# A two-layer attention and state-space kernel: first group's transposes into other banks and later, output rows asked for earlier, one dt product into a score buffer

## The chip, the cores and the metric

The kernel runs on one core of a Trainium2 chip. A core has five engines that run side by side, each with a queue of its own that is worked off in order: TensorE (PE; its weight loads are shown as PEld), VectorE (DVE), ScalarE (ACT), GpSimd (POOL) and SyncE (SP), which in this kernel issues most of the DMA transfers. Matrix products are written to PSUM, eight banks of 512 fp32 columns on 128 partitions; DVE and ACT read them from there into SBUF. The metric is the device time of one execution in microseconds (us).

## The reference

The model has two layers on a latent grid of 1024 tokens and a context of 256 tokens, 1024 features each. Layer 0 is gated windowed attention with 16 heads on 4 key heads, layer 1 a bidirectional state-space scan (Mamba-2) with 8 groups of 4 heads. Both are of the form below.

```
shift, scale, gate = adaln(c, w_ada[i], b_ada[i])
u = rms_normalize(h) * (1.0 + scale) + shift
y = mixer(u, uc)
h = h + gate * y
```

The attention mixer ends with `(o * silu(g)) @ w_out`. The scan's front is a product, a convolution over five neighbours in time, and a step size per head:

```
z, xbc, dt_raw = split(h @ w_in)
xbc = silu(centred_depthwise_conv(xbc, conv_w, conv_b))
xs, bm, cm = split(xbc)
dt = softplus(dt_raw + dt_bias)
```

In each group the scan runs over chunks of 128 tokens, forwards and backwards; its states start from the final states of the context.

## The kernel before, in words

Activations lie transposed, features on the partitions and tokens in the free dimension, in three parts (`TT`): part 0 and part 1 are the first and last 512 latent tokens, part 2 the 256 of the context. Every fp32 operand x is split into a high part and a remainder (`uH` and `uL` for activations, `wh` and `wl` for weights), and a product is three matmuls, high by high, high by low and low by high (`mm3`, lines 238 to 240). A weight tile comes by DMA into `wr`; ACT makes `wh` (line 221 or 1141), POOL or DVE makes `wl` (line 223 or 1145). The program is written as one stream of Python calls; a scheduler with a simulated clock then orders each engine's instructions by readiness and priority, and `issue_after` ties an instruction to one before it on its engine.

**Attention** (`attention`, lines 818 to 961). Units of one key head and one block of 128 queries are worked off in three phases: part 2, part 0, part 1. `att_front` makes the scores in the S buffers (two, of two banks each) and asks for the unit's gate `sgt`; `att_back` transposes the probabilities and multiplies with the values (lines 793 to 800), calling `tick` after each block of keys. Each tick may call `advance`, which takes one step of a generator from the list `fill` of the phase, as filler for TensorE: in phases 2 and 0 the projections of q and gate of part 1 (`qg1`), in phase 1 the output projections of parts 2 and 0 (`out_steps`). `cur` is the running generator, `nxt` the one whose weights have been asked for. `tick` paces the steps: after `seen` of `count` ticks the share `seen/count` of the `total` steps is to be done; phase 1 has 97 steps and 76 ticks. An output tile (`one`, line 847) asks for its weights, yields, asks for its row `h1` (line 854, two buffers; eight for part 1), makes the product in 4 or 8 steps, adds the gated product to the row (line 858), stores it (859) and sums its squares. `norm` (868) turns the sums into 1/rms on all partitions: `sums` on TensorE, scale and power, a diagonal matrix on DVE (line 378) and the spreading product with ones (line 380), copied by ACT (382). `mod` (874) reloads a row (879) into an `h1` buffer and makes `uH` and `uL` from it (`modulate`, lines 299 to 301). Between phases 0 and 1 the pool of the projections closes and the pool `op` of the output rows opens (line 936).

In the attention stage the PSUM tile `pj` has one buffer: a second product in `pj` starts when the first has been read.

**After attention** (lines 943 to 961) the eight output tiles of part 1 follow one another, alternating between `pj` and S; then the two products with the dt weights (`dt_raw`, which adds the bias on ACT, line 1031, into `dts`), and the norm and modulation of part 1.

**The scan's front** (`front`, line 1128). For each group four weight tiles are worked off in the order bT, first and second half of x, cT. Each makes a product of 1024 columns in an accumulator `raw` (tag pj2, two buffers, line 1212); all but cT also make one of 256 columns for the context in `psD` (one bank, line 1197). In the first group the third dt product (1222) and the chain of dt steps (`dt_chain`) come in between. The steps behind a product wait in the queue `post`: the convolution's `taps` (1111, 1115), `silu` (1126, 1124), and `natural` (line 1160), which transposes the result on TensorE (1166) and has ACT copy it into SBUF (1167). `natural` writes the transposes over `raw` or `psD` again, or, where `apart` is set, into a `psX` buffer (three banks, which the scan uses from the first slot on, and which the dt steps use in the first group); in `before` only the second half of x is `apart`. Its steps fall due LATE (3.0 us) or, apart, LAST (6.8 us) of TensorE cost later. The chain `states` (1300), which carries the states over the chunks, starts when the second half of x is done.

Of the kernel before, what the change touches and what calls it, by code (L numbers as in the profile page):

```python
# [17 lines left out]
P = 128  # L18
# [95 lines left out]
class Kernel:  # L114
# [251 lines left out]
    def rstd_n(self, pool, pn, n, width, size=512, rout=None, dout=None, scalar=False):  # L366

        nc, t, ps = self.nc, self.t, self.psA
        nb = n // P
        rc = t(pool, [P, 4], F32, "rc", 2)[:, :nb]  # L370
        nc.scalar.activation(rc, pn[:, :nb], AF.Identity, bias=self.eps, scale=1.0 / width)
        nc.gpsimd.tensor_tensor(rc, rc, self.half.broadcast_to([P, nb]), op=ALU.pow)
        dg = t(*(dout or (pool, [P, 512], F32, "sqt"))).rearrange("p (b n) -> p b n", b=4)[:, :nb]
        if scalar:
            for b in range(nb):
                nc.scalar.activation(dg[:, b], self.ident, AF.Copy, scale=rc[:, b : b + 1])
        else:
            nc.vector.tensor_tensor(dg, self.ident.unsqueeze(1).broadcast_to([P, nb, P]), rc.unsqueeze(2).broadcast_to([P, nb, P]), op=ALU.mult)
        pr = t(ps, [P, 512], F32, self.ptag)
        self.spread_mm = nc.tensor.matmul(pr[:, :n], self.ones, dg.rearrange("p b n -> p (b n)"), start=True, stop=True)  # L380
        r = t(*(rout or (pool, [P, size], F32, f"rr{size}")))[:, :n]
        nc.scalar.copy(r, pr[:, :n])
        return r
# [434 lines left out]
    def attention(self, c0, ckv):  # L818
# [23 lines left out]
        def out_steps(i):  # L842
# [4 lines left out]
            def one(m):  # L847
                p = self.po
                w = self.load_halves(a["wo"][m], nc.gpsimd, i == 1)
                yield  # L850
                h1 = t(self.o1, [P, n], F32, "h1k") if i == 1 else t(p, [P, n], F32, "h1")
                if i == 1:
                    st[m] = h1
                nc.sync.dma_start(h1, self.xin(i)[m * P : (m + 1) * P, :])
                out = []
# [11 lines left out]

            def norm():
                p = self.po
                rout = (p, [P, n], F32, "ut" if i == 2 else "sqa")  # L870
                st["r"] = self.rstd_c(p, st["acc"], n, D, rout=rout, dout=(p, [P, 512], F32, "dg0"))
                self.alloc_u(i)
# [9 lines left out]
            def fin():  # L882
                yield
                for f in steps:
                    f()
# [22 lines left out]
        def advance(i, after):  # L908
            nonlocal cur, nxt
            with self.tc.high_priority(offset=-300), self.tc.issue_after(after):  # L910
                if cur is None:
                    cur = nxt or fill[i].pop(0)()
                    if nxt is None:
                        next(cur)
                    nxt = None
                    if fill[i]:
                        nxt = fill[i].pop(0)()
                        next(nxt)
                if next(cur, "end") == "end":
                    cur = None  # L920
# [8 lines left out]
        for x, (i, j, b) in enumerate(units):  # L929
            if oH[i] is None:  # L930
                if i == 1:
# [4 lines left out]
                    self.po = self.pool("op", ctx=c0)  # L936
                n = TT[i][1]
# [12 lines left out]
        with ExitStack() as c1:  # L950
# [6 lines left out]
            for i, lo in ((2, 256), (0, 0)):  # L957
                n = TT[i][1] // 2
                self.dt_raw(self.dts[:, lo : lo + n], self.proj(ps, self.wdt, i), n)
            for _ in steps[-1]():  # L960
                pass
# [166 lines left out]
    def front(self, g, st, post, first=None, dt=None):  # L1128
# [50 lines left out]

        tiles = [(16 + g, "bT"), (2 * g, 0), (2 * g + 1, 1), (24 + g, "cT")]  # L1180
# [7 lines left out]
        for n, (x, kind) in enumerate(tiles):  # L1188
# [4 lines left out]
            def ctx():  # L1193
# [6 lines left out]
                post.extend(self.taps(x, cr, acc, 0, CTX, CTX) + self.silu(cr, acc) + natural(cr, acc, [(st[nat[0]][2], 0, 2)], nat[1], 2))  # L1200
# [25 lines left out]
            if nat:  # L1226
                post.extend(natural(raw, acc, [(st[nat[0]][i], 4 * i, 4 * i + 4) for i in range(2)], nat[1], 8, kind == 1))
# [4 lines left out]
            post.append((LAST if kind == 1 else LATE, [done]) if nat else done)  # L1232
# [582 lines left out]
```

## Time and profile before

| | |
|---|---|
| median of three runs | 1773.27 us (1772.14 to 1777.59) |
| profiled execution: time | 1775.01 us |
| profiled execution: span in the profile | 1773.2 us |
| mean granted TensorE clock | 0.997 |
| moved by DMA | 225.53 MB, mean 127 GB/s |

| stage | from, us | to, us |
|---|---|---|
| norm, q, k, v, gate of layer 0 | 0 | 250 |
| attention, phases 2 and 0 | 250 | 490 |
| attention, phase 1 | 490 | 690 |
| output tiles of part 1, dt products | 690 | 734 |
| front of the first group | 734 | 826 |
| eight groups of scan, with the next front or the output product beside it | 826 | 1660 |
| rest of the output product and final norm | 1660 | 1773 |

The page's first part gives for each engine its busy time, its share of the span, and its instructions. A row of the table of stretches gives the stretch, its length, then for PE, PEld, DVE, ACT and POOL the busy us with the number of instructions, then the granted clock of TensorE (1.00 is full speed), the share of the DMA engines and GB/s. A row of waits gives engine, tile and line of the one who waited, engine, tile and line of the one who released it, the total in us, how often, and the longest. A row of a timeline gives the start and length in us, engine, line, operation, out<-in with sizes and the count, and in brackets the idle time before it with what ended it; SPq is SP's DMA queue. In a row of groups the numbers behind the bar are busy us, mean ns of one, and the idle time before them.

### The profile page before, as it was taken

To read this page: it belongs to the slowest core of one execution; us is meant where nothing else is said; L and a number is where in the kernel's file an instruction comes from. 1 tells how busy PE (TensorE), PEld (TensorE's weight loads), DVE (VectorE), ACT (ScalarE), POOL (GpSimd) and SP (SyncE) were. 2 spreads that over 40 slices of the span, in tenths; PEclk is the share of its full clock that TensorE was granted. 3 is DMA by queue.
4 is the path that set the end of the run, shared out by engine and by line. 5 is a ranking of instruction groups with operands and counts; after the bars stand their busy time and mean duration, and the time that the engine had idled before them with its cause. 6 is when DMAs were issued, how large, how long until landed. Compare 5 with 4: busy or idle time off the path is not lost.

```text
span 1773.2 us, 29238 instructions
## 1 busy us (share of the span) xinstructions
PE 1736.4 (98%) x10413; PEld 1503.1 (85%) x10413; DVE 1198.7 (68%) x2119; ACT 871.4 (49%) x1902; POOL 794.9 (45%) x1066
## 2 busy tenths in 40 slices
PE   9999999999999999999999999999999999999997
PEld 6897788888888887778898998989889898988887
DVE  5744436788867775694876867677686767876634
ACT  4522247777777774452544434344444434544522
POOL 3231046555565545104454554636455363554321
PEclk9999999999999999999999999999999999999999
DMA  9478856444455436222223232332333333655533
GB/s 361 169 211 271 287 146 144 102 113 97 113 153 131 119 101 223 75 69 63 76 78 96 74 92 71 86 79 74 91 81 82 83 83 80 182 164 168 179 104 119
DMA packets 211389, 225.53 MB, mean 127 GB/s; under 512 B 15788, under 2 KB 149036, under 8 KB 211244
## 3 DMA queue, kind: packets, MB, share of 16 engines
q1 hardware_dynamic: 177180, 205.02, 38.9%
q0 software_dynamic: 34064, 18.65, 5.8%
q8 instruction: 82, 1.34, 0.3%
q14 instruction: 63, 0.52, 0.1%
HBM read 188.78 MB, written 35.13 MB: 126 GB/s over the span
## 4 chain that ended last, share of the span: by engine, by line
PE 85%; DVE 7%; DMA 3%; ACT 2%; issue 2%; POOL 0%; SPq 0%; DVEq 0%; ACTq 0%; POOLq 0%
PE pj L1212 19%; PE pj L1246 10%; PE pj L1647 7%; PE pj L238 7%; PE pj L239 6%; PE pj L240 6%; PE psD L1197 4%; PE psX L1399 3%; PE pt L793 3%; PE psD L1315 2%; PE pv L800 2%; PE pv L799 2%; PE S L767 2%; PE psX L1368 2%; PE psX L1367 2%
## 5 line engine op out<-in xcount | busy, mean ns | idle before, releaser
L238 PE MATMUL pj<-uH,wh 128*128 128x512 f32 (+1 forms) x680 | 244.3, 360 | 4.2 <-DVE h L858 2.5
L239 PE MATMUL pj<-uL,wh 128*128 128x512 f32 (+1 forms) x680 | 231.0, 340 | 0.4 <-POOL uL L816 0.4
L240 PE MATMUL pj<-uH,wl 128*128 128x512 f32 (+1 forms) x680 | 230.2, 339 | 1.1 <-POOL wl L223 1.1
L1212 PE MATMUL pj<-uH,wh 128*128 128x512 f32 x512 | 173.6, 411 | 1.2 <-ACT bn L1167 1.2
L1212 PE MATMUL pj<-uH,wl 128*128 128x512 f32 x512 | 170.2, 403 | 0.0
L1212 PE MATMUL pj<-uL,wh 128*128 128x512 f32 x512 | 168.1, 402 | 0.0
L1290 POOL TENSOR_TENSOR xw<-xn,dtdec 128x256 f32<-128x256 f32 x144 | 95.6, 665 | 159.2 <-PE psD L1315 75.8
L238 PEld LDWEIGHTS pj<-uH,wh 128*128 128x128 f32 x680 | 129.6, 191 | 28.7 <-ACT wh L221 5.3
L1246 PE MATMUL pj<-wh,uH 128*128 128x256 f32 x512 | 150.5, 294 | 0.0
L1246 PE MATMUL pj<-wl,uH 128*128 128x256 f32 x512 | 150.2, 293 | 0.0
L1246 PE MATMUL pj<-wh,uL 128*128 128x256 f32 x512 | 149.9, 293 | 0.0
L798 DVE TENSOR_TENSOR pl<-pt,ph 128x512 fp32r<-128x512 f32 x168 | 115.0, 689 | 48.5 <-ACT ph L797 46.9
L240 PEld LDWEIGHTS pj<-uH,wl 128*128 128x128 f32 x680 | 129.3, 191 | 16.8 <-POOL wl L223 1.6
L239 PEld LDWEIGHTS pj<-uL,wh 128*128 128x128 f32 x680 | 130.0, 191 | 10.6 <-issue 1.1
L772 DVE CUSTOM_DVE_ANT_0 sm<-S,mask,nsink 128x640 f32<-128x640 f32 (+2 forms) x160 | 119.1, 773 | 23.4 <-PE S L768 16.9
L223 POOL TENSOR_TENSOR wl<-wr,wh 128x512 fp32r<-128x512 f32 x74 | 96.9, 1312 | 80.6 <-ACT wh L221 73.0
L1431 ACT ACTIVATE uT<-psX,nw 128x128 f32<-128x128 f32 x128 | 46.6, 364 | 170.7 <-PE psX L1430 169.8
L774 ACT ACTIVATE sm<-sm,nm 128x640 f32<-128x640 f32 (+2 forms) x160 | 118.6, 743 | 18.2 <-DVE nm L772 17.6
L797 ACT CAST ph<-pt 128x512 fp32r<-128x512 f32 x168 | 97.9, 585 | 50.9 <-PE pt L793 48.3
L221 ACT CAST wh<-wr 128x512 fp32r<-128x512 f32 (+1 forms) x116 | 74.7, 648 | 87.9 <-PE pj L239 66.1
L1212 PEld LDWEIGHTS pj<-uH,wl 128*128 128x128 f32 x512 | 95.8, 188 | 20.0
L1212 PEld LDWEIGHTS pj<-uL,wh 128*128 128x128 f32 x512 | 95.3, 188 | 19.3
(352 smaller groups left out, 4930.8 us busy)
## 6 DMA issues: line engine op xcount, KB each, us to landing
wr<-w_x SPq DMA_DIRECT2D x32, 512.0 KB, 3.8
M<-acs SPq DMA_DIRECT2D x64, 256.0 KB, 5.2
bw<-acs SPq DMA_DIRECT2D x64, 256.0 KB, 5.3
wr<-w_sk SPq DMA_DIRECT2D x24, 512.0 KB, 4.0
wr<-wg SPq DMA_DIRECT2D x40, 256.0 KB, 5.0
qs<-q POOLq DMA_DIRECT2D x40, 256.0 KB, 3.8
wada<-w_ada SPq DMA_DIRECT2D x16, 512.0 KB, 8.5
wr<-wq SPq DMA_DIRECT2D x32, 256.0 KB, 3.4
```

What stands on the lines that cost most here:

```text
L223: (eng or nc.vector).tensor_tensor(l, raw, h, op=ALU.subtract)
L238: self.nc.tensor.matmul(ps, lh, rh, start=first and i == 0, stop=False)
L239: self.nc.tensor.matmul(ps, lh, rl, start=False, stop=False)
L240: self.last_mm = self.nc.tensor.matmul(ps, ll, rh, start=False, stop=last and i == n - 1)
L772: nc.vector.tensor_tensor_reduce(out=sm[:, :W], in0=Sv, in1=self.mask[:, m0 : m0 + W], scale=-SCALE, scalar=self.nsink[:, 4 * j + r : 4 * ...
L774: nc.scalar.activation(sm[:, :W], sm[:, :W], AF.Exp, bias=nm[:, r : r + 1], scale=-1.0, accum_out=sums[:, r : r + 1])
L797: nc.scalar.copy(ph, ptf)
L798: nc.vector.tensor_sub(pl, ptf, ph)
L1212: self.pe = nc.tensor.matmul(raw[:, 512 * i : 512 * i + 512], l[:, k, :], r[i][:, k, :], start=k + y == 0, stop=k == KT - 1 and y == 2)
L1246: self.pe = nc.tensor.matmul(pj[:, c], l, r[:, k, :], start=c % 2 + q + k + y == 0, stop=c % 2 == 1 and q == 1 and k == 3 and y == 2)
L1290: nc.gpsimd.tensor_tensor(xw, X(st, c).rearrange("p (r h) -> p r h", r=R), self.dtdec[:, c, hd(d, g)].unsqueeze(2).broadcast_to([P, R, HP] ...
L1647: self.pe = nc.tensor.matmul(banks[x], l[:, z, sl], r, start=k == 2 * qs[0] and y == 0, stop=k == 2 * qs[-1] + 1 and y == 2)
```

## The change

It has four parts.

- `rstd_n` is split into `rstd_d` (up to the diagonal) and `rstd_r` (spread and copy). For part 1, `fin` now makes the sums and the diagonal at its first step. That step is taken right behind the first dt product, and the second dt product goes to an S buffer.
- An output tile has one more yield, so that its row `h1` can be asked for before its product. `advance` takes two steps of the next generator in phase 1, so weights and row are asked for one tile ahead. At a phase's last tile it takes the first generator of the next phase, so the weights are asked for across the boundary.
- When phase 1 begins, the row of its first tile is asked for behind the opening of the pool `op`, and `seen[1]` starts at -3 and not at 0.
- In the first group (`early`) all transposes of bT and x, and those of their context parts, go to `psX` buffers and fall due LAST and not LATE; so does the mark that a tile is done.

```diff
--- before.py
+++ after.py
@@ -364,8 +364,11 @@
         return self.rstd_n(pool, self.sums(acc, n), n, *args, **kw)
 
     def rstd_n(self, pool, pn, n, width, size=512, rout=None, dout=None, scalar=False):
-
-        nc, t, ps = self.nc, self.t, self.psA
+        return self.rstd_r(pool, self.rstd_d(pool, pn, n, width, dout, scalar), n, size, rout)
+
+    def rstd_d(self, pool, pn, n, width, dout=None, scalar=False):
+
+        nc, t = self.nc, self.t
         nb = n // P
         rc = t(pool, [P, 4], F32, "rc", 2)[:, :nb]
         nc.scalar.activation(rc, pn[:, :nb], AF.Identity, bias=self.eps, scale=1.0 / width)
@@ -376,7 +379,11 @@
                 nc.scalar.activation(dg[:, b], self.ident, AF.Copy, scale=rc[:, b : b + 1])
         else:
             nc.vector.tensor_tensor(dg, self.ident.unsqueeze(1).broadcast_to([P, nb, P]), rc.unsqueeze(2).broadcast_to([P, nb, P]), op=ALU.mult)
-        pr = t(ps, [P, 512], F32, self.ptag)
+        return dg
+
+    def rstd_r(self, pool, dg, n, size=512, rout=None):
+        nc, t = self.nc, self.t
+        pr = t(self.psA, [P, 512], F32, self.ptag)
         self.spread_mm = nc.tensor.matmul(pr[:, :n], self.ones, dg.rearrange("p b n -> p (b n)"), start=True, stop=True)
         r = t(*(rout or (pool, [P, size], F32, f"rr{size}")))[:, :n]
         nc.scalar.copy(r, pr[:, :n])
@@ -845,13 +852,14 @@
             st = {}
 
             def one(m):
-                p = self.po
                 w = self.load_halves(a["wo"][m], nc.gpsimd, i == 1)
                 yield
+                p = self.po
                 h1 = t(self.o1, [P, n], F32, "h1k") if i == 1 else t(p, [P, n], F32, "h1")
                 if i == 1:
                     st[m] = h1
                 nc.sync.dma_start(h1, self.xin(i)[m * P : (m + 1) * P, :])
+                yield
                 out = []
                 yield from self.proj_g(out, ps, w, oH, oL, i, "S" if i == 1 and m % 3 else "pj", parts={0: PARTS, 1: 1, 2: CPARTS}[i])
                 pj = out[0]
@@ -865,10 +873,15 @@
                     nc.scalar.activation(sq, h1, AF.Square)
                     (nc.vector if i == 1 else nc.gpsimd).tensor_tensor(st["acc"], st["acc"], sq, op=ALU.add)
 
+            def sums():
+                p = self.po
+                st["dg"] = self.rstd_d(p, self.sums(st["acc"], n), n, D, dout=(p, [P, 512], F32, "dg0"))
+
             def norm():
+                if "dg" not in st:
+                    sums()
                 p = self.po
-                rout = (p, [P, n], F32, "ut" if i == 2 else "sqa")
-                st["r"] = self.rstd_c(p, st["acc"], n, D, rout=rout, dout=(p, [P, 512], F32, "dg0"))
+                st["r"] = self.rstd_r(p, st["dg"], n, rout=(p, [P, n], F32, "ut" if i == 2 else "sqa"))
                 self.alloc_u(i)
 
             def mod(k):
@@ -880,6 +893,9 @@
                 self.modulate(1, h, st["r"], i, k)
 
             def fin():
+                if i == 1:
+                    sums()
+                yield
                 yield
                 for f in steps:
                     f()
@@ -913,9 +929,12 @@
                     if nxt is None:
                         next(cur)
                     nxt = None
-                    if fill[i]:
-                        nxt = fill[i].pop(0)()
+                    f = fill[i] or fill[{2: 0, 0: 1, 1: 1}[i]]
+                    if f:
+                        nxt = f.pop(0)()
                         next(nxt)
+                        if i == 1:
+                            next(nxt)
                 if next(cur, "end") == "end":
                     cur = None
             done[i] += 1
@@ -934,6 +953,8 @@
                     i = 1
                     cq.close()
                     self.po = self.pool("op", ctx=c0)
+                    next(nxt)
+                    seen[1] = -3
                 n = TT[i][1]
                 oH[i] = t(self.up, [P, KT, n], F32R, f"uH{i}")
                 oL[i] = t(self.up, [P, KT, n], F32R, f"uL{i}")
@@ -956,8 +977,11 @@
             self.dt_setup()
             for i, lo in ((2, 256), (0, 0)):
                 n = TT[i][1] // 2
-                self.dt_raw(self.dts[:, lo : lo + n], self.proj(ps, self.wdt, i), n)
-            for _ in steps[-1]():
+                self.dt_raw(self.dts[:, lo : lo + n], self.proj(ps, self.wdt, i, "pj" if i else "S"), n)
+                if i:
+                    last = steps[-1]()
+                    next(last)
+            for _ in last:
                 pass
         BUFS.update(wr=2, wh=2, wl=2)
         if "u1" in self.dump:
@@ -1177,6 +1201,8 @@
                 steps += [lambda x=x: out[x]() for x in range(len(dst))]
             return [(LAST if apart else LATE, steps)]
 
+        early = g == 0
+
         tiles = [(16 + g, "bT"), (2 * g, 0), (2 * g + 1, 1), (24 + g, "cT")]
         st["xn"] = [t(p, [P, 4, R * HP], F32, "xn4") for _ in range(2)] + [t(p, [P, NCC, R * HP], F32, "xn2")]
         st["bn"] = [t(p, [P, 4, NST], F32, "bn4") for _ in range(2)] + [t(p, [P, NCC, NST], F32, "bn2")]
@@ -1197,7 +1223,7 @@
                         self.pe = nc.tensor.matmul(cr, l[:, k, :], r[2][:, k, :], start=k + y == 0, stop=k == KT - 1 and y == 2)
                         yield N256
                 acc = t(pf, [P, CTX], F32, "cctx")
-                post.extend(self.taps(x, cr, acc, 0, CTX, CTX) + self.silu(cr, acc) + natural(cr, acc, [(st[nat[0]][2], 0, 2)], nat[1], 2))
+                post.extend(self.taps(x, cr, acc, 0, CTX, CTX) + self.silu(cr, acc) + natural(cr, acc, [(st[nat[0]][2], 0, 2)], nat[1], 2, early))
 
             if nat and g + n == 0:
                 yield from ctx()
@@ -1224,12 +1250,12 @@
                     post.append(lambda: self.dt_tail(draw, post, *dt))
             post.extend(self.taps(x, raw, acc, 0, LAT, LAT) + self.silu(raw, acc))
             if nat:
-                post.extend(natural(raw, acc, [(st[nat[0]][i], 4 * i, 4 * i + 4) for i in range(2)], nat[1], 8, kind == 1))
+                post.extend(natural(raw, acc, [(st[nat[0]][i], 4 * i, 4 * i + 4) for i in range(2)], nat[1], 8, early or kind == 1))
 
             def done(kind=kind, acc=acc):
                 st[kind] = acc
 
-            post.append((LAST if kind == 1 else LATE, [done]) if nat else done)
+            post.append((LAST if early or kind == 1 else LATE, [done]) if nat else done)
         need(w)
         w0, w = w, loads[-1]()
         post.extend(w["steps"])
```

## The prediction

> **What bounds the kernel now.** I read the page's busy shares first, then the table of busy time by stretch, then TensorE's waits, and last the timelines of single engines around each wait.
>
> ```profile
> span 1773.2 us, 29238 instructions
> PE 1736.4 (98%) x10413; PEld 1503.1 (85%) x10413; DVE 1198.7 (68%) x2119; ACT 871.4 (49%) x1902; POOL 794.9 (45%) x1066
> ```
>
> TensorE is the bound: it is without work for 1773.2 - 1736.4 = 36.8 us. The number of matmuls does not change here, so the change can only take idle time away, add some, or move the clock. The stretches around the edits (columns: stretch, its length, then busy us of PE, PEld, DVE, ACT, POOL, the granted clock, DMA):
>
> ```profile
> 480.00:490.00 10.00, 10.00 (x68) 8.85 (x67) 8.83 (x19) 6.15 (x12) 4.87 (x6) 1.00 0.19 61
> 490.00:498.00 8.00, 4.86 (x26) 3.29 (x25) 4.20 (x9) 4.61 (x13) 4.86 (x7) 1.00 0.77 181
> 499.00:502.00 3.00, 3.00 (x15) 2.90 (x15) 1.48 (x4) 1.83 (x5) 1.28 (x1) 0.50 0.18 54
> 502.00:503.00 1.00, 1.00 (x8) 1.00 (x8) 0.43 (x1) 0.62 (x1) 0.00 (x0) 0.81 0.00 0
> 685.00:695.00 10.00, 7.84 (x31) 5.04 (x30) 7.55 (x9) 5.12 (x9) 5.79 (x5) 1.00 0.74 272
> 760.00:780.00 20.00, 18.32 (x96) 15.28 (x95) 20.00 (x21) 9.62 (x11) 0.00 (x0) 1.00 0.09 27
> 860.00:1540.00 680.00, 680.00 (x4248) 611.99 (x4247) 496.97 (x810) 304.25 (x692) 348.97 (x486) 1.00 0.33 87
> ```
>
> The steady groups (860 to 1540) hold no idle TensorE time, so nothing is to be had there. Three places are left: the switch to the last attention phase near 490, the dt products near 725, and the first group's front at 760 to 785. Of TensorE's waits between 680 and 840 two that the edits do not aim at (us in total, times, longest):
>
> ```profile
> PE psD L1315 <- DVE hb L1327: 1.2, 2, 0.6
> ...
> PE pj L240 <- POOL wl L223: 1.1, 1, 1.1
> ```
>
> The others of that list are single waits on L1031 and L1167, and their rows follow at their places.
>
> **The dt products.** Both write the single pj bank, and the bias step (L1031) must empty it in between; psD of the new stage waits for it again.
>
> ```profile
> 725.95 0.50 PE L238 MATMUL pj<-uH,wdth 128*128 128x512 f32 x1 [0.96 <-ACT cacc L1031]
> ...
> 731.65 1.02 PE L380 MATMUL pt<-dg,ones 128*128 128x512 f32 x2
> 733.80 0.38 PE L1197 MATMUL psD<-uH,wh 128*128 128x256 f32 x1 [1.13 <-ACT cacc L1031]
> ```
> ```profile
> 731.85 1.90 ACT L1031 ACTIVATE cacc<-pj,db 32x256 f32<-32x256 f32 x4 [4.50 <-PE pj L240]
> ```
>
> With the second product in an S buffer, it follows the sums at once: 0.96 us gone. pj is then empty from 725.95 on (the second product starts on it there), and psD, which by its wait lies on that bank, need not wait for the second bias step: 1.13 us gone. The split norm adds no instruction; it asks for the diagonal before the second product instead of after it, and the spread (L380) still stands behind that product. What is late next is the modulation of the last 512 columns: its copy (L382) follows the four bias activations on ScalarE, so it moves by 0.96 only, and its first uL (L301, at 739.70) comes at 738.7, done by 739.5; TensorE asks for it behind the first 24 matmuls, at 742.2 - 2.1 = 740.1. It holds by 0.6 us. Gain 2.1; if psD waits for the S buffer instead, 0.96.
>
> **The first group's transposes.** Same transposes and copies, in psX and 6.8 instead of 3.0 us of TensorE work behind their tile. What they held was the accumulator (raw, two of them) and psD, both needed by the next tiles.
>
> ```profile
> 767.85 1.09 PE L1166 MATMUL pj<-ident,bT 128*128 128x128 f32 x8 [0.52 <-DVE bT L1124]
> 770.10 0.73 PE L1212 MATMUL pj<-uH,wh 128*128 128x512 f32 x2 [1.16 <-ACT bn L1167]
> 782.64 0.39 PE L1197 MATMUL psD<-uH,wh 128*128 128x256 f32 x1 [1.14 <-ACT xn L1167]
> ```
> ```profile
> 766.63 1.16 DVE L1124 SCALAR_TENSOR_TENSOR bT<-pj,bT 128x1024 f32<-128x1024 f32 x1
> ...
> 777.03 0.42 DVE L1124 SCALAR_TENSOR_TENSOR cctx<-psD,cctx 128x256 f32<-128x256 f32 x1
> ...
> 781.67 1.21 DVE L1124 SCALAR_TENSOR_TENSOR cacc<-pj,cacc 128x1024 f32<-128x1024 f32 x1
> ```
>
> The three waits are 0.52 + 1.16 + 1.14 = 2.82 us. Now a buffer comes free with its last SiLU product (L1124). For bT that is 766.63 + 1.16 = 767.79; TensorE is through at 767.85 - 0.52 = 767.33, so 0.46 stays. The next 48 matmuls and the 24 of the context follow; two rows of the chain of waits give their price:
>
> ```profile
> 733.80 3.14 PE psD L1197 x24
> 736.94 5.47 PE pj L1212 x24
> ```
>
> 767.8 + 10.9 = 778.7, psD is free since 777.45; with 3.1 for the context and 1.1 for bT's transposes TensorE is at 782.9 when it wants the second accumulator, free at 781.67 + 1.21 = 782.88. So gain 2.82 - 0.46 = 2.4. Bounds: 2.82 above; 0 below, because DVE is full there (20.00 of 20) and may only hand the wait to the next tile. I take 2.4, since the three L1124 rows fix the release times without a new DVE instruction.
>
> **The output rows.** The switch at 490, first the queue of SP, then DVE, then TensorE, then the first context tile's matmuls:
>
> ```profile
> 490.53 1.08 SPq L655 DMA_DIRECT2D q<-ql  x2
> 492.10 0.38 SPq L749 DMA_DIRECT2D sgt<-sg  x1
> 492.53 2.17 SPq L854 DMA_DIRECT2D h<-ctxT  x2
> ```
> ```profile
> 497.13 0.48 DVE L858 SCALAR_TENSOR_TENSOR h<-pj,mod,h 128x256 f32<-128x256 f32 x1 [2.71 <-DMA h<-ctxT]
> ```
> ```profile
> 497.66 0.39 PE L238 MATMUL pj<-uH,wh 128*128 128x256 f32 x1 [2.15 <-DVE h L858]
> ```
> ```profile
> L240 PE MATMUL pj<-uH,wl x8: 278/282/283, 484.5 to 488.9; 128*128 128x256 f32 x8
> ```
>
> The first tile's product is ready at 489, its row h1 is asked for at 492.53 behind q's stores and sgt, and DVE stands still on it with the next scores and pl behind it; the second tile needs the one pj bank, so TensorE stands too. Between 490 and 498 it is idle 8 - 4.86 = 3.14 us, and right after it runs 3 us at a granted clock of 0.50 and 1 us at 0.81: 1.5 + 0.19 = 1.69 us more. The place costs 4.83 us. In the changed kernel the row is asked for at the switch, past sgt (0.4 us earlier) but still behind q's stores; what really moves is the counter, set to -3: three ticks pass without a projection, so L858 comes three ticks later, when the row is there. The price: 24 matmuls (3.1 us by the row above) leave a stretch where DVE is busy 8.83 of 10 and TensorE has little else. Bounds: 4.83 if everything else fills in, -3.1 if the empty ticks idle and nothing is saved. I take 4.83 less three quarters of 3.1 (an estimate: DVE's gaps there, 1.17 of 10 us, let about a quarter of the work be made up): 2.5.
>
> [...]
>
> The weights asked for across the other phase boundary cost and bring nothing: TensorE shows no wait for wr, wh or wl between 240 and 510. The three ticks of filler come back at the end of the phase: 97 x 73/76 rounds up to 94, so 3 of 97 steps are left for the flush, among the 2.16 us idle of 685 to 695. I take 0, between -1 and +1.1 (the wl wait). The state chain's 1.2 (L1315) moves with its stage: 0, between -1.2 and +1.2.
>
> **The sum.** 2.1 + 2.4 + 2.5 = 7.0 us. The profiled execution took 1775.01 with 1.8 around its span, so one like it would show a span of 1766.2 and 1768.0; it lies 1.7 above the median of the three runs, inside their spread. The median becomes 1773.3 - 7.0 = 1766.3.
>
> **Rivals.** First, the empty ticks cost what they save: gain 4.5, time 1768.8. For it: DVE is as full before 490 as TensorE; against it: DVE's own 2.71 us wait does go. Second, the front's waits only move along DVE's full stretch, and of 2.4 just the 0.5 of the first is won: 7.0 - 1.9 = 5.1, time 1768.2. Third, the empty ticks idle TensorE as long as 490 to 498 does now, and the clock falls a second time at the same price: 4.5 - 1.7 = 2.8, time 1770.5. [...] Against it: the granted clock in the page's forty slices shows no fall that costs a tenth of a slice, though waits of 1 us are common.
>
> ```profile
> PEclk9999999999999999999999999999999999999999
> ```
>
> Fourth, and on the other side: h1 has two buffers, and the modulations of the context and of the first 512 columns (sixteen reloads, L879) use them too. A row asked for a tile ahead holds one buffer always, so the reloads may queue until the last out tile is stored.
>
> ```profile
> 669.75 0.33 SPq L859 DMA_DIRECT2D h<-h  x1
> ```
> ```profile
> h<-h SPq DMA_DIRECT2D x16, 256.0 KB, 2.7
> ```
> ```profile
> L299 DVE SCALAR_TENSOR_TENSOR h<-h,mod,sqa 128x512 f32<-128x512 f32 x8 | 7.7, 972 | 3.6 <-DMA h<-h 3.6
> L301 DVE SCALAR_TENSOR_TENSOR uL<-h,mod,uH 128x512 fp32r<-128x512 f32 x8 | 7.6, 956 | 0.3
> ```
> ```profile
> 710.62 0.75 DVE L301 SCALAR_TENSOR_TENSOR uL<-h,mod,uH 128x512 fp32r<-128x512 f32 x1
> ```
>
> A load and two DVE steps are 2.7 + 0.97 + 0.96 = 4.6 us. Sixteen of them through one buffer from 669.8 end at 743; the second dt product needs the last uL at about 730. Late by 13, less the 7.0: 1779. It decides once the last L301 of that half, now 710.62, passes 730. Against it: two buffers are free after the last store, which halves it to 707.
>
> **How the numbers follow.** Chances: forecast 0.55 (its own range 1764 to 1768.5), first rival 0.20, second 0.10, third 0.08, fourth 0.07. The range's low end is all upper bounds together (2.1 + 2.8 + 4.8 + 1.1 = 10.8): 1762.4; its high end takes in the third rival with 2 us of the small bounds: 1772.5. A measurement of this kernel tells about 0.3%, 5.3 us, from no change, so faster begins at 1768.0: nine tenths of the forecast, a quarter of the first rival, near half of the second, 0.50 + 0.05 + 0.05 with a little for gains that I left at 0, 0.63. Slower is the fourth rival, 0.07; 0.30 between.
>
> **What would show it.** Right: no wait of L238 or L1197 on L1031, none of L1212 or L1197 on L1167 before 800, no stretch after 490 with a clock of 0.50, and the steady groups as long as before. Wrong: idle TensorE time between 480 and 495 that grew by 3 us, L1212 of the cT tile waiting for L1124, or uL (L301) of the first half ending after 730.

## The result, and the profile after

| | before | after |
|---|---|---|
| median time | 1776.68 us (1772.14 to 1777.88, 9 runs) | 1782.39 us (1777.93 to 1787.18, 9 runs) |
| profiled execution: time | 1775.01 us | 1778.86 us |
| profiled execution: span | 1773.2 us | 1777.2 us |

The ratio of the times is 1.0033, 95% interval 1.0023 to 1.0044: the change makes the kernel about 5.9 us slower. It was forecast 7 us faster. One execution of all that follow, the profiled one of e10, ran at a mean granted clock of 0.65 and took 2442.12 us; no comparison uses it, and the table of stages has no row of e10. The head of the page of after (total busy time, share, instructions by engine):

```profile
span 1777.2 us, 29247 instructions
...
PE 1740.4 (98%) x10413; PEld 1506.0 (85%) x10413; DVE 1194.6 (67%) x2119; ACT 872.1 (49%) x1902; POOL 793.2 (45%) x1066
```

TensorE is idle for 1777.2 - 1740.4 = 36.8 us, exactly as before. What grew is its busy time, by 4.0 us with the same 10413 matmuls: more of them ran at a lower clock (mean granted clock 0.993, before 0.997). Where, the stretches of after show (stretch, its length, busy us of PE, PEld, DVE, ACT, POOL, granted clock, DMA):

```profile
480.00:490.00 10.00, 8.62 (x49) 6.50 (x48) 9.38 (x21) 7.59 (x18) 4.62 (x7) 1.00 0.15 40
490.00:498.00 8.00, 8.00 (x61) 7.51 (x60) 6.18 (x15) 6.01 (x13) 4.98 (x7) 1.00 0.67 149
...
720.00:740.00 20.00, 18.04 (x93) 14.97 (x92) 12.94 (x19) 12.41 (x22) 1.60 (x1) 0.91 0.37 118
760.00:780.00 20.00, 19.15 (x99) 15.98 (x98) 19.94 (x22) 11.36 (x14) 0.00 (x0) 1.00 0.10 29
780.00:800.00 20.00, 15.58 (x84) 12.67 (x82) 12.91 (x20) 10.49 (x37) 1.17 (x2) 0.94 0.53 135
800.00:820.00 20.00, 18.32 (x115) 16.12 (x116) 9.04 (x11) 5.09 (x10) 7.08 (x12) 0.80 0.06 14
...
860.00:1540.00 680.00, 680.00 (x4240) 611.63 (x4238) 496.90 (x811) 305.14 (x693) 347.53 (x483) 1.00 0.33 87
```

The switch at 490 is better than before, the front at 760 to 780 too. New are a clock of 0.91 at the dt products and a place from 780 to 820 with 6.1 us idle (1.1 before) and clocks of 0.94 and 0.80.

Two executions differ by some us ahead of the first scores, so places are compared from common marks on TensorE's timeline: the first scores of attention (S), the first matmul of the first dt product, the first matmul of the bT product of the first group, and the first matmul of the z product of the second group. Before, then after:

```profile
247.88 0.28 PE L768 MATMUL S<-kHH,qs 128*128 128x256 f32 x1
721.24 0.28 PE L238 MATMUL pj<-uH,wdth 128*128 128x256 f32 x1
736.77 0.40 PE L1212 MATMUL pj<-uH,wh 128*128 128x512 f32 x1
902.12 0.47 PE L1246 MATMUL pj<-wh,uH 128*128 128x256 f32 x1
```
```profile
246.35 0.28 PE L775 MATMUL S<-kHH,qs 128*128 128x256 f32 x1
718.48 0.39 PE L238 MATMUL pj<-uH,wdth 128*128 128x256 f32 x1 [0.32 <-DVE h1k L866]
734.46 0.40 PE L1238 MATMUL pj<-uH,wh 128*128 128x512 f32 x1
905.81 0.47 PE L1272 MATMUL pj<-wh,uH 128*128 128x256 f32 x1
```

Attention and output rows take 473.36 us before and 472.13 after, the dt products 15.53 and 15.98, the first group 165.35 and 171.35. What comes behind is 871.1 and 871.4 us long. Together with the 1.5 us by which the first scores came earlier this makes the 4.0 us between the spans: -1.5 - 1.2 + 0.45 + 6.0 + 0.3. So the loss lies in the first group: 6.0 us, where 2.4 were to be won.

**The first group.** Two of the three waits that the forecast aimed at are gone: none of L1238 (the product in `raw`) or L1223 (psD) on L1191 (the copy of the transposes) is left. The third has grown: the bT tile's transposes wait 0.85 us, where it was 0.52 before and 0.46 were forecast. The new wait comes 33 us later. The timelines of TensorE, ACT and DVE of after (the row at 792.76 is the second half of the first x tile's transposes):

```profile
765.88 1.09 PE L1190 MATMUL psX<-ident,bT 128*128 128x128 f32 x8 [0.85 <-DVE bT L1148]
...
792.76 0.60 PE L1190 MATMUL psX<-ident,cacc 128*128 128x128 f32 x4
...
794.55 0.58 ACT L1191 COPY xn<-psX 128x512 f32<-128x512 f32 x1
795.02 1.22 ACT L1135 ACTIVATE cacc<-pj,cb,cw 128x1024 f32<-128x1024 f32 x1
...
793.58 1.23 DVE L1169 TENSOR_TENSOR wl<-wr,wh 128x1024 fp32r<-128x1024 f32 x1 [3.00 <-ACT wh L1165]
797.24 1.27 DVE L1139 SCALAR_TENSOR_TENSOR cacc<-pj,cw,cacc 128x1022 f32<-128x1022 f32 x1
798.42 0.22 DVE L1100 TENSOR_TENSOR vd<-psX,vf 128x64 f32<-128x64 f32 x1
...
798.70 0.69 PE L1190 MATMUL psX<-ident,cctx 128*128 128x128 f32 x2 [2.85 <-DVE vd L1100]
```

The convolved tile of x lies in `cacc`, which has two buffers. One of them holds the dt steps `dts` at this time, the other the first x tile, and it comes free only when the last of its transposes has run. Those are due later now: the last four start 58.3 us behind the bT mark, where before all eight started 48.1 us behind it. Until then the second x tile's convolution cannot start. ACT's first step of it (L1135) runs at 795.02, 60.6 us behind the bT mark; before, it ran 50.2 us behind it. The two rows of before:

```profile
784.88 1.03 PE L1166 MATMUL pj<-ident,cacc 128*128 128x128 f32 x8
...
786.92 1.22 ACT L1111 ACTIVATE cacc<-pj,cb,cw 128x1024 f32<-128x1024 f32 x1
```

Meanwhile DVE waits (3.00 us ahead of `wl`), and then it has the convolutions of cT and x at once, with the small step `vd` that empties a psX bank among them. TensorE stands on that bank for 2.85 us, with the states and the z product behind it in its queue, and when it goes on its clock has fallen to one half until 808 (granted clock 0.50 from 798 to 808).

**The dt products.** The waits on the bias step are gone, as forecast. In their place stands one of the spread on the diagonal, and the clock falls. After, the engines' timelines and then one stretch:

```profile
725.35 0.95 PE L360 MATMUL pt<-ones,sqa 128*128 128x1 f32 x8
...
726.33 0.27 ACT L374 ACTIVATE rc<-pt,eps 128x4 f32<-128x4 f32 x1 [0.18 <-PE pt L360]
...
726.68 1.60 POOL L375 TENSOR_TENSOR rc<-rc,half 128x4 f32<-128x4 f32 x1 [8.77 <-ACT rc L374]
...
728.32 0.69 DVE L381 TENSOR_TENSOR dg<-ident,rc 128x512 f32<-128x512 f32 x1 [0.91 <-POOL rc L375]
...
729.06 1.69 PE L387 MATMUL pt<-dg,ones 128*128 128x512 f32 x2 [1.96 <-DVE dg L381]
```
```profile
730.00:731.00 1.00, 1.00 (x4) 0.48 (x4) 0.00 (x0) 0.21 (x1) 0.00 (x0) 0.50 0.26 102
```

With no bank to wait for, the second product was put ahead of the sums. Only three of its 24 matmuls are left behind them, and the chain of sums, scale, power, diagonal and spread (3.7 us from 725.35 to 729.06) has only these three to run under.

### The profile page after: what moved, and what is told of

It reads as the page before. It is cut to its first block, busy times and chain, and to the rows that moved or that the text cites. A ratio compares the mean times of both kernels' runs of the same rounds, so it can differ in the third digit from the quotient of the medians.

```text
span 1777.2 us, 29247 instructions
## 1 busy us (share of the span) xinstructions
PE 1740.4 (98%) x10413; PEld 1506.0 (85%) x10413; DVE 1194.6 (67%) x2119; ACT 872.1 (49%) x1902; POOL 793.2 (45%) x1066
## 4 chain that ended last, share of the span: by engine, by line
PE 88%; DVE 6%; issue 2%; ACT 2%; DMA 1%; POOL 1%; DVEq 0%; SPq 0%; ACTq 0%; POOLq 0%
PE pj L1238 19%; PE pj L1272 10%; PE pj L1673 7%; PE pj L238 7%; PE pj L239 7%; PE pj L240 7%; PE psD L1223 4%; PE pt L800 3%; PE psX L1425 3%; PE psD L1341 2%; PE pv L807 2%; PE pv L806 2%; PE S L774 2%; PE psX L1394 2%; PE psX L1393 2%
## 5 line engine op out<-in xcount | busy, mean ns | idle before, releaser
L1238 PE MATMUL pj<-uH,wh 128*128 128x512 f32 x512 | 173.2, 410 | 0.0
L1238 PE MATMUL pj<-uH,wl 128*128 128x512 f32 x512 | 170.6, 403 | 0.0
L1238 PE MATMUL pj<-uL,wh 128*128 128x512 f32 x512 | 167.8, 402 | 0.0
L1238 PEld LDWEIGHTS pj<-uH,wl 128*128 128x128 f32 x512 | 95.7, 188 | 19.9
L1238 PEld LDWEIGHTS pj<-uL,wh 128*128 128x128 f32 x512 | 95.3, 188 | 19.4
```

What stands on the lines that cost most here:

```text
L1238: self.pe = nc.tensor.matmul(raw[:, 512 * i : 512 * i + 512], l[:, k, :], r[i][:, k, :], start=k + y == 0, stop=k == KT - 1 and y == 2)
```

## The experiments

Twelve kernels in three batches, each timed against the kernel before on its own chip. The stages of all profiled executions, in us, from the marks above (the row of a mark is the first matmul of that kind on TensorE's timeline):

| kernel | first scores at | to first dt product | to bT product | sum of both | to 2nd z product | to the end |
|---|---|---|---|---|---|---|
| before | 247.88 | 473.36 | 15.53 | 488.89 | 165.35 | 871.1 |
| after | 246.35 | 472.13 | 15.98 | 488.11 | 171.35 | 871.4 |
| e1, first group alone | 248.06 | 471.13 | 15.50 | 486.63 | 172.52 | 872.2 |
| e3, due early again | 246.68 | 473.03 | 17.27 | 490.30 | 168.24 | 871.4 |
| e4, own buffer | 249.22 | 472.96 | 17.42 | 490.38 | 165.01 | 872.9 |
| e2, without first group | 246.99 | 472.00 | 16.22 | 488.22 | 165.35 | 870.8 |
| e9, dt alone | 247.53 | 472.18 | 16.74 | 488.92 | 165.63 | 870.8 |
| e6, e2 with sums first | 247.25 | 472.52 | 13.94 | 486.46 | 165.65 | 870.8 |
| e5, rows alone | 246.66 | 472.82 | 19.24 | 492.06 | 166.29 | 871.4 |
| e7, e2 without head start | 246.72 | 473.58 | 14.50 | 488.08 | 165.36 | 871.3 |
| e8, both mended | 251.64 | 472.13 | 13.92 | 486.05 | 166.50 | 870.9 |
| e11, both mended, no rows | 247.55 | 471.38 | 13.02 | 484.40 | 166.42 | 870.8 |
| e12, e8 again | 246.41 | 472.10 | 13.92 | 486.02 | 163.36 | 871.4 |

Four matmuls of the second dt product lie ahead of the dt mark in after, e2, e3 and e4, and one in e7 and e9 (0.23 us each, by their starts), so the first dt column of these kernels holds less work; the sum of both columns is free of this.

### The first group

e1 puts the first group's part alone on the kernel before.

```diff
+        early = g == 0
...
-natural(cr, acc, [(st[nat[0]][2], 0, 2)], nat[1], 2))
+natural(cr, acc, [(st[nat[0]][2], 0, 2)], nat[1], 2, early))
...
-nat[1], 8, kind == 1))
+nat[1], 8, early or kind == 1))
...
-LAST if kind == 1 else LATE
+LAST if early or kind == 1 else LATE
```

> The kernel before with the first group's transposes alone changed (psX, due LAST). Both theories (held accumulator: the transposes that fall due late keep one of the two cacc buffers, so the next tile's convolution cannot start; psX contention: transposes and dt steps share three banks and TensorE's queue stands behind them) put the whole loss here: TensorE idle for 6 us or more within a stretch of 25 us around 795, the clock at 0.50 behind it, time 5 to 9 us above the kernel before. Rival (the scheduler's order elsewhere): within 2 us of the kernel before.

1781.18 us, ratio 1.0037 (1.0025 to 1.0049). The wait of 2.86 us on `vd` is there again, and the stage is 7.2 us longer than before: the loss of the whole change lies in this part.

e3 keeps the psX banks but lets the transposes fall due LATE again, except those of the second x tile; e4 keeps the later due time and gives the second x tile's convolution a spare buffer of the bT tile.

```diff
-            return [(LAST if apart else LATE, steps)]
+            return [(LAST if apart and (o or not early) else LATE, steps)]
```
```diff
-            acc = t(pf, [P, LAT], F32, "cacc") if nat and kind != "bT" else t(p, [P, LAT], F32, kind)
+            acc = t(p, [P, LAT], F32, "bT") if early and kind == 1 else t(pf, [P, LAT], F32, "cacc") if nat and kind != "bT" else t(p, [P, LAT], F32, kind)
```

> The changed kernel, the first group's transposes in psX but due 3.0 us behind their tile instead of 6.8 (the second x tile stays at 6.8). Held accumulator: the buffer is given back 3.8 us earlier, the second x tile's convolution starts near 787 instead of 795, most of the stall goes: 4 to 6 us faster than before the change. psX contention: the same nine uses of three banks stand closer together, the stall stays at 5 us or more, and the time stays above the kernel before.

> The changed kernel with the first group's second x tile convolved in the idle second bT buffer; transposes still in psX and due at 6.8 us. Held accumulator: its first convolution step no longer waits for the first x tile's transposes and starts within 3 us of its product's end (near 780 to 786), TensorE idles under 2 us between 780 and 810, time 4 to 6 us below the kernel before. psX contention: convolution early, but TensorE still waits 3 us or more for psX near 795, time above the kernel before.

e3: 1778.2 us, ratio 1.0009 (0.9998 to 1.0019). By the ratios that is 4.3 us below after and not below before. The stall at 795 is gone, and another stands ahead of it:

```profile
787.36 1.71 PE L1190 MATMUL psX<-ident,cacc 128*128 128x128 f32 x8 [3.39 <-DVE cacc L1148]
```

The second x tile's convolution starts 52.7 us behind the bT mark (789.72), between the 50.2 of before and the 60.6 of after. The first x tile's transposes now reach TensorE before DVE has finished their tile. So the due time has to lie between two ends: too early and TensorE waits for the tile, too late and the tile's buffer is kept from the next one.

e4: 1775.19 us, ratio 1.0001 (0.9988 to 1.0014). The place that cost 6.1 us has no idle time left:

```profile
780.00:790.00 10.00, 10.00 (x58) 8.76 (x57) 9.88 (x12) 7.12 (x10) 0.00 (x0) 1.00 0.16 40
790.00:800.00 10.00, 10.00 (x59) 8.67 (x59) 8.69 (x13) 5.03 (x14) 1.04 (x1) 1.00 0.69 114
800.00:810.00 10.00, 10.00 (x86) 9.95 (x85) 7.20 (x9) 6.74 (x28) 2.57 (x4) 1.00 0.36 121
```

The second x tile's convolution starts 44.2 us behind the bT mark (783.77, the mark at 739.60). The due times and the psX banks are those of after, only the buffer is another: it was the held accumulator, not the banks and not the lateness by itself. The time was expected 4 to 6 us below before and is level with it; against after it is 5.7 us less by the ratios. The two stages ahead of the first group take 1.5 us more in e4 than before (490.38 and 488.89).

e10 is e1 with that buffer.

> The kernel before with the first group's part alone, and the second x tile's convolution of that group in a spare buffer of the bT tile. Theory of the held accumulator: the stall of 5.3 us near 795 to 804 is gone, the states' chain near 830 waits 1.75 us instead of 1.29, and the time is 1 to 3 us below before, 7 us below the same part without the spare buffer. Rival (transposes ahead of the later products are dear by themselves): no stall, but the time not below before, since the clock falls at the states' chain.

1773.87 us, ratio 0.9987 (0.9978 to 0.9997): 2.3 us below before by the ratio, where e1 lay 6.6 us above. That is as expected.

### The dt products

e2 is the change without the first group's part, e9 the dt part alone on the kernel before (the output rows' edits undone too), e6 is e2 with the second product tied behind the sums.

```diff
-        early = g == 0
+        early = False
```
```diff
-                self.dt_raw(self.dts[:, lo : lo + n], self.proj(ps, self.wdt, i, "pj" if i else "S"), n)
+                with ExitStack() as cs:
+                    if i == 0:
+                        cs.enter_context(self.tc.issue_after(self.last_sum.ins))
+                    pj = self.proj(ps, self.wdt, i, "pj" if i else "S")
+                self.dt_raw(self.dts[:, lo : lo + n], pj, n)
```

> The changed kernel with the first group's transposes as before; rows ahead and the dt products stay. All theories of the first group: no stall near 800, and what is left is the output rows (+2.8 won) and the dt products (0.5 lost): 1.5 to 3 us faster than the kernel before. Rival (rows and dt products lose by themselves): not faster than before.

> The kernel before with the dt part alone: second dt product in a score buffer, sums written ahead of the norm; rows and first group as before. Theory of the exposed chain: the place from the start of the first dt product to the first product of the layer (12.56 us in the profile of before) becomes 11 to 12.5 us, with a wait of the spread on the diagonal of 1.5 to 2.5 us where the two waits on the dt turn stood, and the time stays within 1 us of before. Rival (the part wins its 2.1 us when it stands alone, and it was the rows that made the chain late): no wait of the spread over 0.5 us, 10.5 us for the place, 2 us faster.

> The change without the first group's part, and with the second dt product held behind the sums of the norm on TensorE's queue. Theory of the exposed chain: the wait of the spread on the diagonal (2.41 us without this hold) falls below 0.5 us, no half clock between 728 and 734, and the time is 2 to 3 us below the change without the first group's part, about 4 us below before. Rival (the scalar engine's turn, not the place of the sums, sets the diagonal): the wait of the spread stays over 1.5 us and the time is that of the change without the first group's part.

e2: 1774.78 us, ratio 0.9998 (0.9985 to 1.0012), so the 1.5 to 3 us expected of it did not come. e9: 1773.48 us, ratio 0.9994 (0.9985 to 1.0002), about 1 us from before, as expected of the exposed chain. e6: 1774.6 us, ratio 0.9985 (0.9974 to 0.9996), 2.7 us below before, where about 4 were expected. The spread's row in e2, e9 and e6:

```profile
729.96 2.08 PE L387 MATMUL pt<-dg,ones 128*128 128x512 f32 x2 [2.41 <-DVE dg L381]
```
```profile
731.08 1.76 PE L387 MATMUL pt<-dg,ones 128*128 128x512 f32 x2 [2.14 <-DVE dg L381]
```
```profile
723.42 1.02 PE L360 MATMUL pt<-ones,sqa 128*128 128x1 f32 x8 [0.57 <-DVE sqa L874]
...
729.98 1.02 PE L387 MATMUL pt<-dg,ones 128*128 128x512 f32 x2
```

The wait comes with the dt part, also without the rows (e9), and goes with the order of two things on TensorE's queue (e6). How long it is varies: in e7 below it is 1.46 us, and the clock stays at 1.00 there. With the sums first, the stage takes 13.94 us and not 16.22, and both stages together 486.46 and not 488.22. One thing was unforeseen: with a bank of its own the second product also fills gaps of the last output tiles where it isn't tied; in after its first four matmuls run at 712.

### The output rows

e5 has the rows' part alone on the kernel before. e7 is e2 without the head start of three ticks.

```diff
-                    seen[1] = -3
```

> The kernel before with the output rows alone: the rows asked for a step ahead, the first step of the fills taken at the switch; first group and dt products as before. Working theory (the rows win what the switch near 490 wins, the dt part nets about nothing and the first group loses about 7 us): the switch idles 1.7 us instead of 3.1 and shows no stretch at half clock, the first dt product starts about 2.8 us earlier, the two waits on the dt turn (0.93 and 1.13 us) are back, time about 2.5 us below before. Rival (the rows' gain is used up by the weights that then come sooner or by the half's later waits): the first dt product earlier, but the end of the run the same as before within 0.5 us.

> The change without the first group's part and without the head start of three steps for the second half's fills at the switch. If the head start is what spaces the loads at the switch, the idle time of TensorE between 480 and 500 is back to 3 us or more, with a stretch at half clock, and the time is 1.5 to 2.5 us above the change without the first group's part. If asking for the rows ahead is enough, the switch idles under 2 us and the time is the same within 0.5 us.

e5: 1778.29 us, ratio 1.0016 (1.0005 to 1.0028), slower than before; both expectations of it had missed that. e7: 1774.83 us, ratio 0.9992 (0.998 to 1.0003), no slower than e2. The idle time at the switch was read rightly, and it is the head start that takes it away: from 480 to 500 TensorE is idle for 2.28 to 3.14 us in the four executions with the rows as before, for 2.52 in e7, which has the rows but not the head start, and for 1.37 to 1.70 in the eight executions with it. But the sum of the first two stages is the same in e7 and e2 (488.08 and 488.22). Two rows of e7, and then, for e12 (with the rows) and e11 (without them, both told below), the stretches of the last attention phase:

```profile
480.00:500.00 20.00, 17.48 (x114) 14.80 (x113) 15.40 (x31) 14.13 (x30) 10.70 (x13) 1.00 0.46 120
...
560.00:640.00 80.00, 78.82 (x454) 66.28 (x454) 62.10 (x131) 59.32 (x131) 44.34 (x63) 1.00 0.47 121
```
```profile
480.00:500.00 20.00, 18.61 (x124) 15.98 (x123) 16.91 (x37) 15.53 (x34) 11.64 (x16) 1.00 0.43 110
500.00:560.00 60.00, 60.00 (x421) 55.51 (x420) 42.40 (x92) 46.40 (x103) 42.16 (x58) 1.00 0.62 155
560.00:640.00 80.00, 75.47 (x427) 62.61 (x428) 60.20 (x124) 55.55 (x124) 41.53 (x59) 1.00 0.45 116
640.00:718.00 78.00, 75.44 (x361) 59.51 (x359) 45.90 (x80) 39.94 (x79) 36.55 (x38) 1.00 0.48 159
```
```profile
480.00:500.00 20.00, 17.72 (x116) 15.05 (x115) 15.47 (x31) 13.51 (x30) 10.58 (x13) 1.00 0.45 114
500.00:560.00 60.00, 59.52 (x411) 54.08 (x409) 42.22 (x89) 45.07 (x99) 42.57 (x59) 1.00 0.56 148
560.00:640.00 80.00, 78.34 (x447) 65.47 (x447) 64.92 (x136) 59.38 (x131) 44.09 (x63) 1.00 0.48 124
640.00:718.00 78.00, 73.84 (x361) 59.04 (x360) 50.18 (x83) 40.62 (x80) 37.39 (x38) 1.00 0.49 156
```

With the rows TensorE is idle for 1.39 + 0 + 4.53 + 2.56 = 8.48 us, without them for 2.28 + 0.48 + 1.66 + 4.16 = 8.58. The hole at the switch is smaller and another one opens 100 us later; the sum stays. The second hole, too, comes with the head start: from 560 to 640 the idle time is 1.66 to 2.04 us with the rows as before, 1.18 in e7, and 3.32 to 4.53 in the eight executions with the head start. In e12 it lies in waits on DVE between 610 and 637 (0.82, 0.68 and 1.26 us the longest). And the modulation of the first 512 columns ends later with the head start, close to the first dt product: at 715.7 in e12 (the row below), at 709.0 in e11 and at 710.0 in e7.

```profile
714.93 0.74 DVE L301 SCALAR_TENSOR_TENSOR uL<-h,mod,uH 128x512 fp32r<-128x512 f32 x1
```

In e5 the dt stage takes 3.7 us more than before. Its first dt product starts 0.5 us earlier behind the first scores, but the bias step stands on ACT behind the split of the next weight tile, which waits for its DMA, and so TensorE waits longer for the one `pj` bank (2.20 us, 0.96 before). Behind that wait the granted clock was 0.50 from 728 to 731, which is 1.5 us more of the 3.7:

```profile
723.87 1.04 ACT L1162 CAST wh<-wr 128x1024 fp32r<-128x1024 f32 x1 [1.62 <-DMA wr<-w_x]
...
726.35 0.50 PE L238 MATMUL pj<-uH,wdth 128*128 128x512 f32 x1 [2.20 <-ACT cacc L1052]
```

### All together

e8 has the whole change, with e4's buffer and e6's order. e11 is e8 with the output rows' edits undone, e12 is e8 once more, on one chip with e11.

```diff
-                    next(nxt)
-                    seen[1] = -3
...
-                    f = fill[i] or fill[{2: 0, 0: 1, 1: 1}[i]]
-                    if f:
-                        nxt = f.pop(0)()
-                        next(nxt)
-                        if i == 1:
-                            next(nxt)
+                    if fill[i]:
+                        nxt = fill[i].pop(0)()
+                        next(nxt)
```

> The whole change, the second x tile's convolution in a spare buffer of the bT tile for the first group, and the second dt product held behind the sums. Theory (held accumulator and exposed chain are the two places where the change loses): no stall between 780 and 810, no wait of the spread over 0.5 us, the z product of the first group starts about 7 us earlier than before, time 5 to 7 us below before. Rival (what is won in the first group is given back at the states' chain, 3 waits of 0.58 us and a clock of 0.94 near 835): time 3 to 4 us below before, the same as the sums-first kernel without the first group's part.

> Both mended parts (spare buffer, second dt product held behind the sums) with the output rows as before. If the rows win nothing (what the switch wins is given back before the first dt product), the time is that of the kernel with both mended parts and the rows within 1 us, and the stretch from the first scores at 247 to the first dt product is 471 to 473.5 us in both. If the rows win what the switch shows, this kernel is 1.5 to 3 us slower than the one with them.

> The kernel with both mended parts and the rows once more, as the other side of the comparison without the rows, on the same chip: 3 to 6 us below before. In its profile the stretch from the first scores to the first dt product tells what the rows win; at the states' chain near 820 to 850 either the clock falls again (then the drop belongs to the order of the work) or stays at 1.00 (then it belongs to the single execution).

e8: 1771.09 us, ratio 0.9977 (0.9965 to 0.999), 4.1 us below before, between its two expectations. e11: 1769.37 us, ratio 0.9965 (0.9952 to 0.9977). e12: 1769.0 us, ratio 0.9968 (0.9956 to 0.9981). The mended versions are faster than both kernels, by 0.35% and 0.32% against before on the last chip. With and without the rows they are the same in time, as expected if the rows win nothing, and the stretch to the first dt product does not favour the rows (472.10 and 471.38). Nor do the two other pairs that differ in the rows alone: e2 and e9 have ratios of 0.9998 and 0.9994, and e5 is slower than before. The second x tile's convolution in e11 starts on ACT 44.2 us behind the bT mark (731.95), ahead of the 50.2 of before:

```profile
776.11 1.19 ACT L1132 ACTIVATE bT<-pj,cb,cw 128x1024 f32<-128x1024 f32 x1
```

## Why the prediction was wrong, point by point

**The first group (+2.4 forecast, -6.0 measured).** Two of the three waits went, 2.30 of the 2.82 us, and the one of bT grew by 0.33. The step that failed is the sentence that what the transposes held "was the accumulator (raw, two of them) and psD". They also read the convolved tile, and so they hold its `cacc` buffer; a later due time keeps it longer. The bound of 0 below followed from that: the list of what is held had no room for a loss. Nor was "the three L1124 rows fix the release times" enough, since they fix when the banks come free, and not the tile in SBUF. e4 shows the cause. With the buffer out of the way, the wait is gone in e4, e8, e11 and e12, and the stage takes 163.36 us in e12: 2.0 less than before, 2.3 less than e6, which differs from it in this part alone. But it takes 165.01, 166.50 and 166.42 us in e4, e8 and e11, where the clock falls at the state chain (0.95, 0.89 and 0.83 from 820 to 840, 1.00 in e12); and that chain, whose change the forecast took as 0, waits 1.75 us in all four and 1.29 in before. By the times e10 lies 2.3 us below before (0.5 to 3.9 by its interval), and e8 is 1.4 below e6 by their ratios on one chip. So the 2.4 was of the right size for a kernel without the held buffer, but not all of it comes in every execution.

**The dt products (+2.1 forecast, -0.5 measured, with four matmuls less in the stage).** Both waits on the bias step went. The step that failed is "it follows the sums at once": the order of the two had been given by the wait itself, and without it the second product went first. The text named what hid the diagonal (the second product) but not what put it there. With the order held, the gain by stage is 15.53 - 13.92 = 1.6 us with the rows and 15.53 - 13.02 = 2.5 without.

**The output rows (+2.5 forecast, nothing measured).** The price of the place was 4.83 us, made of 3.14 idle and 1.69 of half clock. The half clock was of that one execution. In e1, whose code up to there is that of before, the clock stays at 1.00, as it does in e9 and e11, and in the nine kernels with other rows:

```profile
480.00:500.00 20.00, 17.30 (x112) 14.54 (x111) 15.47 (x32) 13.22 (x28) 10.21 (x13) 1.00 0.46 119
...
499.00:502.00 3.00, 3.00 (x23) 2.81 (x22) 2.32 (x5) 2.47 (x6) 2.06 (x2) 1.00 0.14 45
```

Before's idle time was also the longest of these four (3.14 us, 2.28 to 2.90 in the others), so whether it takes that much idle time or is chance stays open. The rest, 1.4 us of idle time at the switch (3.14 in before, 1.70 in after, 480 to 500), was won and then lost again between 560 and 640 (2.04 and 4.18). The step that failed is therefore the 4.83 less three quarters of 3.1: the first number holds 1.69 that other executions of the same code don't show, and the empty ticks cost all of what they save, as the first rival had it, only later: without them, in e7, the late hole is missing. Why it opens between 560 and 640 isn't shown.

**The other rivals.** DVE's full stretch did not take the front's waits back (0.85 us idle from 760 to 780, 1.68 before). The clock fell at two other places (0.50 from 730 to 732 and from 798 to 808), not at the empty ticks (1.00 from 480 to 560). The last uL of the first 512 columns did come later, by 4.3 us (its end moved from 711.4 to 715.6), which is far from the 730 at which the fourth rival begins to decide.

**The signs.** The signs listed as right appeared at the places that they were meant for, and none of those listed as wrong. Taken by the word one failed: "no stretch after 490 with a clock of 0.50" holds for the switch, but not at 730 and 798. All of them watched the old waits or the switch; the two new ones, of the spread on `dg` and of psX on `vd`, were on neither list.

## What to carry to other kernels

When a consumer is moved later, write down every buffer that it reads, not only those that it writes: the input stays held for as long as the output moves. A wait that is taken away may also have been what kept two instructions in order; where the order matters, tie it. And idle time of one execution at lower clock is worth taking into a sum only once a second execution, or other code with the same stretch, shows it again.

## What was not expected of the hardware

The clock behind waits of the same length differed between two executions of one and the same kernel. With the mended first group the state chain waits three times 0.58 us between 820 and 840. Here are the same 20 us of e11, and of e8 and e12, which are one kernel:

```profile
820.00:840.00 20.00, 18.25 (x82) 15.20 (x81) 7.65 (x14) 1.76 (x4) 10.95 (x16) 0.83 0.15 40
```
```profile
820.00:840.00 20.00, 18.25 (x93) 15.24 (x91) 6.92 (x15) 1.97 (x2) 10.66 (x16) 0.89 0.19 53
```
```profile
820.00:840.00 20.00, 18.25 (x95) 15.02 (x95) 10.25 (x22) 4.21 (x11) 12.02 (x17) 1.00 0.19 44
```

The idle time is the same 1.75 us, the clock is 0.83, 0.89 and 1.00, and the stage of e8 is 166.50 - 163.36 = 3.1 us longer than that of e12. At the spread in after, the clock was 0.50 from 730 to 732 behind a wait of 1.96 us. How much idle time it takes for the clock to fall is not shown.

The start varies more than the effects looked for: the first scores come between 246.35 and 251.64 us in the profiled executions, though no kernel differs ahead of them in what it computes. e8's profiled execution has the late start and the lower clock and took 1776.75 us, 5.7 above its median.
